# State space: phase tiles made in the first MLP and loaded, instead of sums in each period

## The chip, the cores and the metric

The kernel runs on one core of a Trainium2 chip. The metric is the device time of one execution in microseconds; the median of several runs is compared. The engines named below are TensorE (PE, with its weight loads as PEld), VectorE (DVE), ScalarE (ACT), GpSimd (POOL) and SyncE (SP), whose queue issues all transfers of this kernel.

## What is computed

The reference is a backbone of two layers over 1024 latent and 256 context tokens of width 1024: layer 0 mixes the tokens by attention, layer 1 by a bidirectional diagonal state space (S5); each mixer is followed by a squared-ReLU MLP. What matters here is the state space:

```
lam_bar = exp(lam * dt)
b_bar = ((lam_bar - 1.0) / lam)[..., None] * b_mat
bu = einsum('gpc,btgc->btgp', b_bar, uc)
a_cum, hs = associative_scan(_linear_combine, (a, bu))      # h[t] = lam_bar * h[t-1] + bu[t]
y = real(einsum('gcp,btgp->btgc', c_mat, hs))
```

lam_bar is complex. The kernel scans with its magnitude alone and takes the rotation out: before the scan the inputs are multiplied by the cosine and sine of a phase that grows with the position, and after the scan the products are turned back with the same cosine and sine. Eight tokens make one step, so that 1280 tokens are 160 positions. The phase of a position is held as a 32-bit integer, in which the full circle is 2 to the 32, and wraps by itself.

## The kernel before

The stages in question are the first MLP's down projection (`mlp0_start`, `mlp0_down`, about 1446 to 1906 us of the span), its end (`mlp0_end`, to about 1938), and the state space (`s5`, to about 2146).

**Down projection.** Eight blocks q of four hidden rows are multiplied into ten token tiles, in groups of tiles (2, 0, 1). After each tile `step` advances a list of background generators, `self.bg`, one or two yields at a time (L1538): first `s5_phases`, then `s5_tables`. `s5_tables` makes the matrices of the state space (loads of `tpd`, `tcd`, `tbd`; products on VectorE, L1138 to L1147; transposes and small products on TensorE, L1153 and L1159) and stores them to `recd`. Outside the stretches named below, a planner that estimates a timeline at build time fixes the order of each engine's instructions and of the transfers on SP's queue; on the chip each engine then runs its own list in that order.

**The phases.** The phase of position 16a + b of a column is the sum of a coarse and a fine table. `s5_phases` (L1198) loads the phase steps (`phd`), makes the fine table B (128 x 128 columns x 16) by doubling on GpSimd (L1207 to L1213), stores it, then makes the coarse table A (128 x 128 x 10) in the same SBUF, and stores it, both into `ptd`. These buffers lie in F from 40 KB on, where `s5_tables` puts its inputs afterwards. In `s5` both tables are loaded back: the columns of the first period into H (A0, B0), the whole, 13 KB a partition, into F from 42.5 KB.

**The state space** runs 16 periods n, of 4 groups of 16 columns each, and three more that only finish. There PE, DVE, ACT and POOL keep the order of the program (`manual`); SP's queue is ordered by the planner. In a period, for each direction d (0 forward, 1 backward):

- `phase` (L1677, the sum at L1681, on GpSimd) adds A and B for 4 columns into a 128 x 640 tile; `trig` (ScalarE, L1685 to L1688) makes sine and cosine of it;
- `inputs` (TensorE, L1701), `rotate` (VectorE, two products from PSUM, L1710), the sum of the two (GpSimd, L1791 forward, L1800 backward), `scan` (VectorE, L1719);
- `back` (L1727): for each direction one product on VectorE and one on GpSimd;
- `outputs` (TensorE, L1733, L1736), the GELU of the period two before (ScalarE, VectorE L1786, L1808), transposes (L1740), and, at periods 8, 10 and 12 to 17, half a segment of the modulation of layer 1 (L247 to L261) from 2 MB of weights loaded two periods earlier.

GpSimd's order in a period is `back` of the period before (backward), the phase sum of the next period forward, L1791, L1800, `back` forward, the phase sum of the next period backward:

```
back(pool, n - 1, 1, 1); phase(n + 1, 0)
pool.tensor_tensor(t1, t1, t2, ALU.add)     # L1791, after rotate(n, 0)
pool.tensor_tensor(t1, t1, t2, ALU.add)     # L1800, after rotate(n, 1)
back(pool, n, 0, 1); phase(n + 1, 1)
```

The tiles of sine and cosine are a ring of three pairs (`phs`). Each period loads its matrices (`load_x`, `load_w`, 2.1 MB) into one of two slots, `load_x` for two periods ahead, `load_w` for one.

Of the kernel before, what the change touches and what calls it, by code (L numbers as in the profile page):

```python
# [70 lines left out]
class Prog:  # L71
# [1125 lines left out]

    def s5_phases(self, o):  # L1198

        nc = self.nc  # L1200
        g = nc.gpsimd.tensor_tensor
        B, P, P16 = (self.fv(x, *d).bitcast(I32) for x, d in ((o, (128, 16)), (o + 8, (128,)), (o + 8.5, (128,))))
        self.dma(self.fv(o + 9, 128), self.phd)
        nc.vector.tensor_copy(P, self.fv(o + 9, 128))

        def fill(T, n, first):
            nc.gpsimd.memset(T[:, :, 0], 0)  # L1207
            g(T[:, :, 1], first, T[:, :, 0], ALU.add)
            m = 2
            while m < n:  # L1210
                g(T[:, :, m], T[:, :, m // 2], T[:, :, m // 2], ALU.add)
                e = min(2 * m, n)
                g(T[:, :, m + 1 : e], T[:, :, 1 : e - m], bcast(T[:, :, m], 2, e - m - 1), ALU.add)  # L1213
                m *= 2

        fill(B, 16, P)
        g(P16, B[:, :, 8], B[:, :, 8], ALU.add)
        self.dma(self.ptd[:, 5 * KB : 13 * KB], B.rearrange("p a b -> p (a b)"))
        yield
        A = self.fv(o, 128, 10).bitcast(I32)  # L1220
        fill(A, 10, P16)
        self.dma(self.ptd[:, 0 : 5 * KB], A.rearrange("p a b -> p (a b)"))
        yield


# [266 lines left out]
    def mlp0_start(self):  # L1492
# [10 lines left out]
        self.yb = Ring([self.PS[:, x : x + 1024] for x in (2048, 3072, 0)])  # L1503
        self.bg = [self.s5_phases(40), self.s5_tables(40, 0, self.bank(3), self.bank(2))]
        self.w2 = {}
# [134 lines left out]
    def s5(self):  # L1640
# [9 lines left out]
        rs = [[self.view(self.U, 52 + 5 * d + 2.5 * i, (4, 160)) for i in range(2)] for d in range(2)]  # L1650
        At, Bt = self.fv(42.5, 128, 10).bitcast(I32), self.fv(47.5, 128, 16).bitcast(I32)
        A0, B0 = self.hv(46, 2, 4, 10).bitcast(I32), self.hv(47, 2, 4, 16).bitcast(I32)
        phs = [(self.fv(x, 4, 160), self.fv(x + 2.5, 4, 160)) for x in (0, 7.5, 24.5)]
        ts = [[(self.fv(x, 4, 160), self.fv((12.5, 20)[d], 4, 160)) for x in ((5, 29.5), (15, 17.5))[d]] for d in range(2)]
# [21 lines left out]

        def phase(n, d):  # L1677

            x0, P = 64 * d + 4 * n, phs[(2 * n + d) % 3][0].bitcast(I32)
            a, b = (At[:, x0 : x0 + 4], Bt[:, x0 : x0 + 4]) if n else (A0[:, d], B0[:, d])  # L1680
            pool.tensor_tensor(P.rearrange("p x (a b) -> p x a b", b=16), bcast(a, 3, 16), bcast(b, 2, 10), ALU.add)  # L1681

        def trig(n, d):
            Ps, Pc = phs[(2 * n + d) % 3]
            act.activation(Pc, Ps.bitcast(I32), AF.Sin, scale=0.5 * UNPHASE)  # L1685
            act.activation(Ps, Ps.bitcast(I32), AF.Sin, scale=UNPHASE)
            act.activation(Pc, Pc, AF.Square)
            act.activation(Pc, Pc, AF.Copy, scale=-2.0, bias=1.0)  # L1688
# [14 lines left out]
        def rotate(n, d):  # L1703
            (Ps, Pc), (t1, t2) = phs[(2 * n + d) % 3], ts[d][n % 2]
            for j, (t, P) in enumerate(((t1, Pc), (t2, Ps))):
# [15 lines left out]
        def back(eng, n, d, j):  # L1721
            Ps, Pc = phs[(2 * n + d) % 3]
            o = cs[d][n % 2][j]
# [22 lines left out]

        for t, c0, w in ((A0, 0, 10), (B0, 5 * KB, 16)):
            self.dma(t, self.ptd[:, c0 : c0 + 128 * w].rearrange("p (d x w) -> p d x w", d=2, w=w)[:, :, 0:4])

        load_x(0)  # L1750
        self.dma(self.fv(42.5, 13 * KB).bitcast(I32), self.ptd)
        load_w(0)
        self.act_set("silu_and_others")
        with self.manual():
            act.activation(U[:, :, 160:192], U[:, :, 0:32], AF.Copy)
            for d in range(2):
                for i in range(2):
                    pool.memset(rs[d][i][:, :, 0:1], 0.0)
            phase(0, 0)
            phase(0, 1)  # L1760
            trig(0, 0)
# [3 lines left out]
            for n in range(19):  # L1765
# [5 lines left out]
                if 1 <= n <= 16:  # L1771
                    back(pool, n - 1, 1, 1)
                if gelu:
                    act.activation(u, y, AF.Square, scale=float(np.sqrt(0.044715)))
                if run:
                    trig(n, 1)
                    decay(n, 1)
                    inputs(n, 0)
                if 0 < n < 15:
                    phase(n + 1, 0)  # L1780
                if run:
# [15 lines left out]
                if run:  # L1797
# [4 lines left out]
                    if n == 0:  # L1802
                        phase(1, 0)
                        trig(1, 0)
# [11 lines left out]
                for i, (a, b) in enumerate(mods):  # L1816
                    if n == b:
                        self.ada_half_products(halves[i % 2 if i > 2 else 0], 1, 2 + i // 2, i % 2, self.PS[:, 1856:1984])
                if n + 1 < 16:
                    phase(n + 1, 1)  # L1820
                if 3 <= n < 19:
# [275 lines left out]
    def run(self):  # L2097
        tc = self.tc
        pool = lambda name, **kw: tc.tile_pool(name=name, bufs=1, **kw)
        with pool("cst") as self.cst, pool("psp", space=bass.MemoryType.PSUM) as psp, \  # L2100
# [12 lines left out]
            self.Ad = [dt(f"Ad{i}", 16, 128, 512) for i in range(7)]  # L2113
            self.phd, self.ptd = dt("phd", 128, 128), drp.tile([128, 13 * KB], I32, name="ptd")
            self.tcd, self.tbd, self.tpd = dt("tcd", 128, 128, 32), dt("tbd", 128, 128, 32), dt("tpd", 128, 128, 34)
# [99 lines left out]
```

## Time and profile before

| | us |
|---|---|
| three runs | 2986.51, 2996.61, 2990.26 |
| median | 2990.26 |
| span of the profiled execution | 2980.2 |
| down projection | 1446 to 1906 |
| its end | 1906 to 1938 |
| state space | 1938 to 2146 |

The profile is of one execution, and its span runs from the first to the last instruction; the page gives no other time for that execution. Times inside the trace count from the start of the span. Busy times are those of an engine's instructions; the granted clock of TensorE is a share of its full speed; the DMA share is the mean busy share of the core's 16 DMA engines. A row of a timeline has its start, its length, engine, line, operation, output and input, and, in brackets, how long the engine stood idle before it and what ended that.

### The profile page before, as it was taken

The numbers are of one execution on the slowest core, as the hardware profiler recorded it, in microseconds if no ns is written. First come the engines' busy times: TensorE is split into PE (matmuls) and PEld (weight loads), VectorE is DVE, ScalarE is ACT, GpSimd is POOL, SyncE is SP. The second block draws the span as 40 slices with busy tenths as digits, with TensorE's granted clock in tenths as the row PEclk, the third lists the DMA queues.
The fourth block names the chain that finished last, engine by engine and source line by source line (L and its number), as shares of the span: only waits on it lengthen the run. The fifth ranks groups of instructions, "written<-read, shape, count | busy, mean of one in ns | idle before, by whom it ended". The sixth has DMA issues, their size and how long they took to land.

```text
span 2980.2 us, 43413 instructions
## 1 busy us (share of the span) xinstructions
PE 2799.0 (94%) x15440; PEld 2335.0 (78%) x15440; DVE 1931.3 (65%) x2782; ACT 1314.3 (44%) x2406; POOL 1066.0 (36%) x923
## 2 busy tenths in 40 slices
PE   6998999999899999999999999688899899999999
PEld 4687887888777787888777778588788678888887
DVE  6356777777763654444577774799733687758566
ACT  3325655555553743333422232367534643334443
POOL 2314666666653600000100001589501543327323
PEclk9999999999999999999999999889999999999999
DMA  9955555555725446322666674568934244467544
GB/s 277 298 171 170 150 171 166 164 168 161 237 86 178 131 151 185 122 96 85 198 178 185 182 225 120 161 177 262 290 112 156 78 145 160 155 197 268 166 135 141
DMA packets 427941, 510.79 MB, mean 171 GB/s; under 512 B 59094, under 2 KB 304076, under 8 KB 426572
## 3 DMA queue, kind: packets, MB, share of 16 engines
q1 hardware_dynamic: 427724, 508.03, 55.8%
q8 instruction: 121, 1.98, 0.3%
q14 instruction: 96, 0.79, 0.1%
HBM read 353.38 MB, written 150.31 MB: 169 GB/s over the span
## 4 chain that ended last, share of the span: by engine, by line
PE 66%; DVE 9%; DMA 9%; issue 5%; POOL 4%; ACT 4%; SPq 2%; DVEq 0%; POOLq 0%; ACTq 0%
PE PS L132 19%; PE PS L134 19%; PE PS L133 19%; SPq L80 2%; PE PS L520 2%; PE PS L1701 2%; ACT F L543 2%; PE PS L1736 1%; DVE F L533 1%; PE PS L566 1%; PE PS L202 1%; DMA R<-Vd 1%; DMA H<-hidd 1%; DVE FD L1719 1%; DMA Kd<-R 1%
## 5 line engine op out<-in xcount | busy, mean ns | idle before, releaser
L132 PE MATMUL PS<-H,R 128*128 128x512 f32 (+1 forms) x840 | 311.4, 377 | 15.2 <-ACT F L579 13.5
L133 PE MATMUL PS<-H,R 128*128 128x512 f32 (+1 forms) x840 | 306.8, 365 | 5.2 <-POOL H L138 5.2
L132 PE MATMUL PS<-H 128*128 128x512 f32 x776 | 303.6, 393 | 3.9 <-ACT H L137 3.9
L134 PE MATMUL PS<-H,R 128*128 128x512 f32 (+1 forms) x840 | 306.3, 366 | 0.0
L133 PE MATMUL PS<-H 128*128 128x512 f32 x776 | 304.3, 392 | 0.0
L134 PE MATMUL PS<-H 128*128 128x512 f32 x776 | 302.6, 391 | 1.6 <-DVE H L138 1.6
L137 ACT ACTIVATE R<-W 128x512 fp32r<-128x512 f32 (+1 forms) x191 | 136.1, 717 | 195.0 <-PE PS L133 137.1
L132 PE MATMUL PS<-R,H 128*128 128x512 f32 x532 | 212.9, 403 | 2.9 <-ACT R L137 1.4
L543 ACT ACTIVATE F<-F,stat 128x1280 f32<-128x1280 f32 x128 | 174.4, 1362 | 84.7 <-DVE F L533 84.4
L134 PE MATMUL PS<-R,H 128*128 128x512 f32 x532 | 208.2, 395 | 1.9 <-DVE H L138 1.9
L133 PE MATMUL PS<-R,H 128*128 128x512 f32 x532 | 209.3, 394 | 0.0
L138 DVE TENSOR_TENSOR H<-W,H 128x512 fp32r<-128x512 f32 (+1 forms) x146 | 142.9, 988 | 101.0 <-ACT H L137 97.5
L138 DVE TENSOR_TENSOR R<-W,R 128x512 fp32r<-128x512 f32 (+1 forms) x154 | 141.7, 926 | 98.6 <-ACT R L137 78.7
L132 PEld LDWEIGHTS PS<-H,R 128*128 128x128 f32 x840 | 161.5, 193 | 41.5 <-ACT F L579 15.0
L533 DVE TENSOR_SCALAR_CACHE_REDUCE F<-PS 128x1280 f32<-128x1280 f32 x128 | 185.1, 1482 | 8.6 <-PE PS L520 8.3
L137 ACT ACTIVATE H<-W 128x512 fp32r<-128x512 f32 (+2 forms) x167 | 107.5, 653 | 180.5 <-PE PS L133 112.6
L133 PEld LDWEIGHTS PS<-H,R 128*128 128x128 f32 x840 | 163.0, 194 | 28.6 <-POOL H L138 6.8
L580 POOL TENSOR_SCALAR R<-F 128x256 fp32r<-128x256 f32 (+1 forms) x128 | 123.9, 968 | 169.3 <-ACT F L579 147.5
L134 PEld LDWEIGHTS PS<-H,R 128*128 128x128 f32 x840 | 162.5, 194 | 26.8 <-issue 1.2
L132 PEld LDWEIGHTS PS<-H 128*128 128x128 f32 x776 | 146.2, 189 | 36.8 <-ACT H L137 4.8
L134 PEld LDWEIGHTS PS<-H 128*128 128x128 f32 x776 | 146.2, 188 | 33.2 <-DVE H L138 2.5
L133 PEld LDWEIGHTS PS<-H 128*128 128x128 f32 x776 | 146.3, 189 | 30.7 <-issue 1.0
(443 smaller groups left out, 7307.6 us busy)
## 6 DMA issues: line engine op xcount, KB each, us to landing
W<-in_mlp_w SPq DMA_DIRECT2D x184, 256.0 KB
Ad<-F SPq DMA_DIRECT2D x112, 256.0 KB
W<-Ad SPq DMA_DIRECT2D x112, 256.0 KB
W<-in_ada_w SPq DMA_DIRECT2D x32, 512.0 KB
W<-in_mlp_w SPq DMA_DIRECT2D x32, 512.0 KB
H<-hidd SPq DMA_DIRECT2D x64, 256.0 KB
U<-in_ada_w SPq DMA_DIRECT2D x32, 512.0 KB
W<-in_s_w_glu SPq DMA_DIRECT2D x64, 256.0 KB
```

Source lines behind the costliest of these rows:

```text
L80: return self.nc.sync.dma_start(out=out, in_=in_)
L132: mm(out, ah, bh, start=first, stop=False, **kw)
L133: mm(out, ah, bl, start=False, stop=False, **kw)
L134: mm(out, al, bh, start=False, stop=last, **kw)
L137: self.nc.scalar.activation(hi, src, AF.Copy)
L138: (lo_eng or self.nc.vector).tensor_tensor(lo, src, hi.bitcast(F32), ALU.subtract)
L202: self.nc.tensor.matmul(acc[32 * j : 32 * j + 32, 0:256], self.scT[:, 2 * k : 2 * k + 32], w[:, 256 * j : 256 * j + 256], start=k == 0, st ...
L520: mm(self.PS[:, 1280 * c + k0 : 1280 * c + k1], Q[:, c, r, qs], K[c][:, k0:k1], start=r == 0, stop=r == 1)
L533: ts(p[c], self.PS[:, 1280 * c : 1280 * c + 1280], 1.0, None, ALU.mult, ALU.min, accum_out=sm[:, c : c + 1])
L543: nc.scalar.activation(p[c], p[c], AF.Exp, bias=sm[:, c : c + 1], scale=-1.0, accum_out=sn[:, 0:1] if c else s0[:, u + 1 : u + 2])
L580: nc.gpsimd.tensor_scalar(hi, t, 1.0, 0.0, ALU.mult, ALU.add)
L1701: mm(b[:, o : o + 160], X[:, d, i, 64 * j : 64 * j + 128], U[:, 4 * n + i, cols], start=True, stop=True)
```

## The change

`s5_phases` keeps both tables in SBUF (A no longer in the place of B) and stores neither. After them it makes all 32 phase tiles on GpSimd, 16 periods by 2 directions, in three buffers in W, and stores each to `ptd`, which becomes 16 x 2 x 128 x 640; it yields after every four tiles. In `s5` the loads of the tables and the sums of `phase` are gone. A load `load_ph` of a finished tile takes their place: the tiles of period 0 ahead of its matrices, (1, 0), (1, 1) and (2, 0) behind them, and in every period n from 1 on those of (n + 1, 1) and (n + 2, 0), after GpSimd's `back` of the period before in the program's order. The ring of sine and cosine grows from three pairs to five, in the place of the tables.

```diff
-    def s5_phases(self, o):
+    def s5_phases(self, o, w):
         nc = self.nc
         g = nc.gpsimd.tensor_tensor
-        B, P, P16 = (self.fv(x, *d).bitcast(I32) for x, d in ((o, (128, 16)), (o + 8, (128,)), (o + 8.5, (128,))))
-        self.dma(self.fv(o + 9, 128), self.phd)
-        nc.vector.tensor_copy(P, self.fv(o + 9, 128))
+        B, A, P, P16 = (self.fv(x, *d).bitcast(I32) for x, d in
+                        ((o, (128, 16)), (o + 8, (128, 10)), (o + 13, (128,)), (o + 13.5, (128,))))
+        self.dma(self.fv(o + 14, 128), self.phd)
+        nc.vector.tensor_copy(P, self.fv(o + 14, 128))
...
         fill(B, 16, P)
         g(P16, B[:, :, 8], B[:, :, 8], ALU.add)
-        self.dma(self.ptd[:, 5 * KB : 13 * KB], B.rearrange("p a b -> p (a b)"))
         yield
-        A = self.fv(o, 128, 10).bitcast(I32)
         fill(A, 10, P16)
-        self.dma(self.ptd[:, 0 : 5 * KB], A.rearrange("p a b -> p (a b)"))
         yield
+        made = Ring([self.wv(w + 2.5 * i, 4, 160).bitcast(I32) for i in range(3)])
+        for n in range(16):
+            for d in range(2):
+                x = slice(64 * d + 4 * n, 64 * d + 4 * n + 4)
+                t = made.next()
+                g(t.rearrange("p x (a b) -> p x a b", b=16), bcast(A[:, x], 3, 16), bcast(B[:, x], 2, 10), ALU.add)
+                self.dma(self.ptd[n, d], t.rearrange("p x n -> p (x n)"))
+            if n % 2:
+                yield
...
-        self.bg = [self.s5_phases(40), self.s5_tables(40, 0, self.bank(3), self.bank(2))]
+        self.bg = [self.s5_phases(40, 0), self.s5_tables(40, 0, self.bank(3), self.bank(2))]
...
-        phs = [(self.fv(x, 4, 160), self.fv(x + 2.5, 4, 160)) for x in (0, 7.5, 24.5)]
+        phs = [(self.fv(x, 4, 160), self.fv(x + 2.5, 4, 160)) for x in (42.5, 47.5, 0, 7.5, 24.5)]
+        ph = lambda n, d: phs[(2 * n + d) % 5]
...
-        def phase(n, d):
-
-            x0, P = 64 * d + 4 * n, phs[(2 * n + d) % 3][0].bitcast(I32)
-            a, b = (At[:, x0 : x0 + 4], Bt[:, x0 : x0 + 4]) if n else (A0[:, d], B0[:, d])
-            pool.tensor_tensor(P.rearrange("p x (a b) -> p x a b", b=16), bcast(a, 3, 16), bcast(b, 2, 10), ALU.add)
+        def load_ph(n, d):
+            self.dma(ph(n, d)[0].bitcast(I32).rearrange("p x n -> p (x n)"), self.ptd[n, d])
...
-        for t, c0, w in ((A0, 0, 10), (B0, 5 * KB, 16)):
-            self.dma(t, self.ptd[:, c0 : c0 + 128 * w].rearrange("p (d x w) -> p d x w", d=2, w=w)[:, :, 0:4])
-
+        load_ph(0, 0)
+        load_ph(0, 1)
         load_x(0)
-        self.dma(self.fv(42.5, 13 * KB).bitcast(I32), self.ptd)
         load_w(0)
+        for n, d in ((1, 0), (1, 1), (2, 0)):
+            load_ph(n, d)
...
-            phase(0, 0)
-            phase(0, 1)
...
                 if 1 <= n <= 16:
                     back(pool, n - 1, 1, 1)
+                for a in ((n + 1, 1), (n + 2, 0)):
+                    if n and a[0] < 16:
+                        load_ph(*a)
...
-                if 0 < n < 15:
-                    phase(n + 1, 0)
...
-                        phase(1, 0)
...
-                if n + 1 < 16:
-                    phase(n + 1, 1)
...
-            self.phd, self.ptd = dt("phd", 128, 128), drp.tile([128, 13 * KB], I32, name="ptd")
+            self.phd, self.ptd = dt("phd", 128, 128), drp.tile([16, 2, 128, 640], I32, name="ptd")
```

## Rows read from the trace of the kernel before

**Rows 1.** The page's chain that ended last, share of the span by engine:

```profile
PE 66%; DVE 9%; DMA 9%; issue 5%; POOL 4%; ACT 4%; SPq 2%; DVEq 0%; POOLq 0%; ACTq 0%
```

**Rows 2.** Windows: us, busy PE PEld DVE ACT POOL, PE clock, DMA share, GB/s

```profile
1446.00:1906.00 460.00, 456.11 (x2237) 364.78 (x2236) 321.97 (x413) 124.10 (x215) 46.22 (x50) 1.00 0.60 176
...
1938.00:2046.00 108.00, 90.79 (x705) 87.14 (x704) 100.94 (x93) 74.27 (x115) 99.98 (x54) 0.92 0.64 192
2046.00:2096.00 50.00, 44.07 (x438) 41.29 (x439) 48.86 (x49) 38.26 (x61) 46.26 (x26) 1.00 0.92 281
2096.00:2136.00 40.00, 35.92 (x424) 34.00 (x422) 37.76 (x43) 23.69 (x39) 29.48 (x16) 0.97 1.04 314
```

**Rows 3.** Timeline of VectorE, period 9 and the start of period 10:

```profile
2046.85 1.54 DVE L1710 TENSOR_TENSOR FD<-PS,FD 128x640 f32<-128x640 f32 x2
...
2050.97 1.48 DVE L1719 TENSOR_TENSOR_SCAN FD<-U,FD 128x640 f32<-128x640 f32 x1
...
2054.27 2.57 DVE L1719 TENSOR_TENSOR_SCAN FD<-U,FD 128x640 f32<-128x640 f32 x1
2056.88 1.58 DVE L1727 TENSOR_TENSOR FD<-FD 128x512 f32<-128x512 f32 x1
2058.38 1.54 DVE L1710 TENSOR_TENSOR FD<-PS,FD 128x640 f32<-128x640 f32 x2
```

**Rows 4.** Timeline of VectorE, the backward product of the last period:

```profile
2130.47 0.69 DVE L1727 TENSOR_TENSOR FD<-FD 128x512 f32<-128x512 f32 x1
```

**Rows 5.** Timeline of GpSimd, the same periods 9 and 15:

```profile
2053.76 1.74 POOL L1727 TENSOR_TENSOR FD<-FD 128x512 f32<-128x512 f32 x1
2055.57 2.34 POOL L1681 TENSOR_TENSOR FD<-FD 128x640 int32<-128x640 int32 x1
...
2059.68 1.28 POOL L1681 TENSOR_TENSOR FD<-FD 128x640 int32<-128x640 int32 x1
...
2130.61 1.69 POOL L1727 TENSOR_TENSOR FD<-FD 128x512 f32<-128x512 f32 x1 [1.52 <-PE PS L1740]
```

**Rows 6.** Timeline of VectorE, waits in the first periods; 1978.94 repeats the second:

```profile
1956.04 1.56 DVE L1710 TENSOR_TENSOR FD<-PS,FD 128x640 f32<-128x640 f32 x2 [2.54 <-ACT FD L1688]
...
1967.41 1.56 DVE L1710 TENSOR_TENSOR FD<-PS,FD 128x640 f32<-128x640 f32 x2 [0.35 <-ACT FD L1688]
```

**Rows 7.** Timeline of VectorE, the start of period 13:

```profile
2095.31 0.82 DVE L1710 TENSOR_TENSOR FD<-PS,FD 128x640 f32<-128x640 f32 x1 [0.97 <-ACT FD L1686]
```

**Rows 8.** Waits of SP's queue, 1930 to 2150: us in total, times, longest

```profile
SPq L80 <- PE PS L1701: 77.0, 18, 14.7
```

**Rows 9.** Timeline of GpSimd, tables of phases in the down projection:

```profile
1447.02 0.53 POOL L1208 TENSOR_TENSOR FD<-FD 128x128 int32<-128x128 int32 x1 [4.02 <-DVE FD L1204]
...
1463.06 0.34 POOL L1207 MEMSET FD<- 128x128 int32 x1 [9.26 <-DMA ptd<-FD]
...
1467.07 0.60 POOL L1213 TENSOR_TENSOR FD<-FD 128x128 int32<-128x128 int32 x1
```

**Rows 10.** Timeline of SP's queue, the stores of the tables and the first load behind:

```profile
1455.35 0.37 SPq L80 DMA_DIRECT2D ptd<-FD  x1
...
1467.70 0.33 SPq L80 DMA_DIRECT2D ptd<-FD  x1
1470.65 0.33 SPq L80 DMA_DIRECT2D FD<-tpd  x1
```

**Rows 11.** Timeline of VectorE, the first product of the state space's tables:

```profile
1473.51 0.76 DVE L1138 TENSOR_TENSOR FD<-FD 128x576 f32<-128x576 f32 x1 [10.67 <-DMA FD<-tcd]
```

**Rows 12.** Timeline of TensorE at the first small product of the tables:

```profile
1477.73 0.46 PE L1159 MATMUL PS<-FD 128*32 128x128 f32 x8 [2.04 <-DVE FD L1140]
...
1478.72 0.63 PE L134 MATMUL PS<-H 128*128 128x512 f32 x1
...
1481.81 0.39 PE L133 MATMUL PS<-H 128*128 128x512 f32 x1
```

**Rows 13.** DMA issues, 2100 to 2150, the largest kind: count, KB each

```profile
W<-recd SPq DMA_DIRECT2D x1, 768.0 KB
```

More of the change, by code (lines that the diff above doesn't have):

```diff
@@ L1650, in s5 @@
         rs = [[self.view(self.U, 52 + 5 * d + 2.5 * i, (4, 160)) for i in range(2)] for d in range(2)]
-        At, Bt = self.fv(42.5, 128, 10).bitcast(I32), self.fv(47.5, 128, 16).bitcast(I32)
-        A0, B0 = self.hv(46, 2, 4, 10).bitcast(I32), self.hv(47, 2, 4, 16).bitcast(I32)
-        phs = [(self.fv(x, 4, 160), self.fv(x + 2.5, 4, 160)) for x in (0, 7.5, 24.5)]
+        phs = [(self.fv(x, 4, 160), self.fv(x + 2.5, 4, 160)) for x in (42.5, 47.5, 0, 7.5, 24.5)]
+        ph = lambda n, d: phs[(2 * n + d) % 5]
         ts = [[(self.fv(x, 4, 160), self.fv((12.5, 20)[d], 4, 160)) for x in ((5, 29.5), (15, 17.5))[d]] for d in range(2)]
@@ L1675, in load_w @@
                 self.dma(b[64 * h : 64 * h + 64, 3072:4096], self.recd[n, 64 - 64 * h : 128 - 64 * h, 1536:2560])
-        def phase(n, d):
-            x0, P = 64 * d + 4 * n, phs[(2 * n + d) % 3][0].bitcast(I32)
-            a, b = (At[:, x0 : x0 + 4], Bt[:, x0 : x0 + 4]) if n else (A0[:, d], B0[:, d])
-            pool.tensor_tensor(P.rearrange("p x (a b) -> p x a b", b=16), bcast(a, 3, 16), bcast(b, 2, 10), ALU.add)
+        def load_ph(n, d):
+            self.dma(ph(n, d)[0].bitcast(I32).rearrange("p x n -> p (x n)"), self.ptd[n, d])
         def trig(n, d):
-            Ps, Pc = phs[(2 * n + d) % 3]
+            Ps, Pc = ph(n, d)
             act.activation(Pc, Ps.bitcast(I32), AF.Sin, scale=0.5 * UNPHASE)
@@ L1703, in rotate @@
         def rotate(n, d):
-            (Ps, Pc), (t1, t2) = phs[(2 * n + d) % 3], ts[d][n % 2]
+            (Ps, Pc), (t1, t2) = ph(n, d), ts[d][n % 2]
             for j, (t, P) in enumerate(((t1, Pc), (t2, Ps))):
@@ L1721, in back @@
         def back(eng, n, d, j):
-            Ps, Pc = phs[(2 * n + d) % 3]
+            Ps, Pc = ph(n, d)
             o = cs[d][n % 2][j]
```

## The prediction

> **What bounds the kernel now.** The chain that ended last is TensorE for two thirds of the span [rows 1]; a gain can only come from a stretch where it isn't, and a loss is certain where it is held up. So the stretches come next [rows 2]. The first MLP's down projection (1446 to 1906) is bound by TensorE, 456 of 460 us, with GpSimd idle nine tenths of it. In the state space (1938 to 2136) VectorE has the most work: 101 of 108, then 49 of 50 and 38 of 40 us, and GpSimd is nearly as full. The same rows show what else is short there: the DMA engines are 0.64 busy first, then 0.92 and 1.04.
>
> One period of the state space, line by line, shows why VectorE is full. Its instructions follow each other without a gap from 2046.85 to 2058.38, 11.53 us a period [rows 3]. Some are far longer than their like. The backward scan takes 2.57 us at 2054.27, the forward one 1.48; the product L1727 at 2056.88 takes 1.58, and 0.69 in the last period, which makes no phase sum [rows 3, 4]. Laid beside GpSimd's line [rows 5], the excess is always what GpSimd's instruction had left to run: the phase sum that began at 2055.57 ran to 2057.91, 1.03 us past the start of the product, which lost 0.89; the product of GpSimd from 2053.76 ran 1.23 us into the scan, which lost 1.09. In the other direction the phase sum takes 2.34 beside the scan, 1.28 alone. So the two engines exclude each other when both read SBUF operands, and a phase sum costs VectorE time though it is on another engine. The sum at 2059.68 stands beside VectorE instructions that read PSUM, 1.54 us a pair as elsewhere, and costs nothing.
>
> **The change, part by part.** (a) *Sums out of the periods.* Of the two a period, the one after GpSimd's L1727 holds VectorE: 1.58 - 0.69 = 0.89 us. It is there in periods 0 to 14, 15 x 0.89 = 13.4 us gained, on the path because VectorE has no gap. What is late next: the scan's 1.09 stays, since GpSimd's L1727 still stands before it. GpSimd's other L1727 now waits for the scan just as VectorE's does; had it gone first, it would hold VectorE 1.1 us instead. In the last period VectorE began first, 2130.47 against 2130.61 [rows 4, 5], so I take the 0.89; ends 0 and 0.89.
>
> (b) *Trigonometry early.* ScalarE no longer waits for sums. Near the start VectorE waited for it 2.54 us, then twice 0.35 [rows 6]: 3.2 us gained; nothing to 3.2.
>
> (c) Where VectorE is not the last, nothing is gained: in period 13 it waited 0.97 us for others [rows 7], so one 0.89 is taken off. (a) to (c): 13.4 + 3.2 - 0.9 = 15.7 us gained.
>
> (d) *Thirty tiles loaded in the periods* (two of the 32 come before). A tile is 128 x 640 x 4 bytes = 0.328 MB, at the 314 GB/s of the full stretch 1.04 us. The three loads of tables that fall away, 1.8 MB in all, lay before 1938. Up to 2046 there are 19 tiles, 20 us, and the engines were idle for 0.36 x 108 = 39 us [rows 2]: hidden. From period 9 on 11 tiles come, 11.5 us, and only 0.08 x 50 = 4.0 us was idle. To shorten this stretch by its six 0.89 = 5.3 us as well, the queue would have to find 11.5 - 4.0 + 5.3 = 12.8 us. The ends are 0 (the loads there run ahead of their use, and the tail goes on into the next stage) and 12.8. I take the middle, 6.4 lost: a tile is asked for one period ahead, about 11 us, and stands behind modulation halves of 2.1 MB, 6.7 us each, so some come late and some not. On SP's queue the second tile of a period waits for GpSimd's L1727 early in that period; the loads behind it wait for TensorE's inputs of the same period or later [rows 8], so that wait costs nothing.
>
> (e) *32 sums and stores in the down projection.* GpSimd's 32 x 1.28 = 41 us stand in 414 idle; even if each held VectorE in full, VectorE has 138 us idle there [rows 2]. The stores, 10.5 MB or 33 us of the queue, stand in 0.40 x 460 = 184 us idle. What is not free is the order. TensorE's order is fixed at build, and the tables' first product stands in it where the planner expected the tables. They use the same SBUF as the phases, so they start when the last phase is stored. Today the sums of table A run from 1463.06 to 1467.67, the store is issued at 1467.70, the loads go out at 1470.65, and VectorE begins at 1473.51 [rows 9 to 11]; TensorE had then waited 2.04 us at the first product, and ran slower right after, 0.63 us a matmul instead of 0.39 [rows 12]. The new chain drops the 9.26 us in which table A waited for B's store and adds 32 sums: 26.5 us from GpSimd's first add (1447.02) to VectorE becomes 26.5 - 9.3 + 32 x 1.36 = 61 us (1.36 is a sum with the gap between instructions). Lateness in proportion is 2.04 x 61 / 26.5 = 4.7, so 2.7 lost more than now. Its ends: a gain of 2.0 if the planner is exact, and 58 lost. For the latter: three buffers, each held for a sum, the issue and the landing of its store. Landing took 2.6 us for 0.66 MB (1467.70 plus 0.33 of issue to 1470.65) and 7.7 us behind other traffic for 1.05 MB (1455.35 to 1463.06) [rows 9, 10]. (1.28 + 0.33 + 2.6) / 3 = 1.4 us a tile, 45 us, hardly above GpSimd's own 43; (1.28 + 0.33 + 7.7) / 3 = 3.1, 99 us, 58 more than the bare sums. I stay by the low end, since a store is half of that A.
>
> (f) *Entry, 1906 to 1938.* Two sums of 1.3 us leave GpSimd, two small loads replace larger ones; the first rotation waits for TensorE, so zero. The cover gone, it would be the tiles' landing, 2 to 3 us.
>
> Sum: -15.7 + 6.4 + 2.7 = -6.6 us. The page gives the span of one profiled execution, 2980.2 us; the median of the three runs is 10.1 us above. The terms are differences within the span and are taken off the median: 2983.7, 0.2% less. A measurement of this kernel can tell some 0.3%, 9.0 us, from no change.
>
> **The rivals.** *The queue keeps up*: (d) is 0, the planner errs little: -15.7 + 2 = -13.7, 2976.6. For it: no wait on a load of the state space stands in today's critical stretch, though the queue is full. Against: eleven tiles more.
>
> *The queue becomes the bound* from period 9: the later stretch gains nothing and grows by 11.5 - 4.0 = 7.5; periods 0 to 8 keep 9 x 0.89 + 3.2 = 11.2; with (e), -11.2 + 7.5 + 2.7 = -1.0, 2989.3. The Trainium skill, page "DMA: Bandwidth & Descriptors", section Bandwidth, asks for transfers of 1 MiB or more for three quarters of the peak; by it a tile of 0.33 MB would cost more than its 1.04 us, which speaks for this rival. The trace speaks against the rule: the full stretch with 314 GB/s is made of smaller loads too, none above 0.8 MB [rows 13].
>
> *The tables come late* (the other side): one mechanism, at TensorE's first table product in the down projection. If the stores' landings pace the ring, TensorE stands still while the tables aren't there. It decides from 9.3 + 9.0 = 18.3 us of lateness, 32 tiles at 1.9 us instead of 1.36; at the middle of its bounds, 30, the time is 2990.3 - 9.3 + 30 = 3011. For it: 2.04 us of just that wait stand in the trace, and TensorE has no slack. Against: landings of 2.6 us.
>
> *It doesn't free VectorE*: GpSimd's L1727 takes the place of the sum before VectorE's. Then (a) is gone: 3.2 - 9.1, 5.9 us lost, 2996. Against it stands which of the two began first [rows 4, 5].
>
> **How the numbers follow.** Forecast 0.42, queue keeps up 0.34, tables late 0.13, queue bound 0.08, not freed 0.03. The forecast's own range is 2978 to 2992; 0.04 of its chance lies under -9 us, 0.02 above +9. Faster by over 0.3%: 0.34 + 0.04 = 0.38. Slower: 0.13 + 0.02, and 0.03 from the bound queue with dearer tiles: 0.18. Within: 0.44. Range: from all of 13.4 + 3.2 with a little of the entry, 2972, to a lateness of 23 us, 3004.
>
> **What would show it.** VectorE's L1727 of the backward direction at 0.69 instead of 1.58, and periods of 10.6 us up to period 8. From period 9 on ScalarE waits for landings of the tiles if (d) is right. The wait before the first L1159 on TensorE tells (e): some 5 us. If that wait is over 18, or the periods stay at 11.5, the forecast is wrong.

## The result and the profile after

| | us |
|---|---|
| before, 6 runs | 2990.53 (2986.51 to 2996.61) |
| changed, 6 runs | 3010.82 (3003.18 to 3021.63) |
| ratio | 1.0074, 95% interval 1.006 to 1.0089 |

The change costs 20.3 us. 2983.7 was forecast, with a range up to 3004: too low, and on the wrong side.

The two profiled executions lie at opposite ends: 2980.2 is below every run of before, 3019.8 belongs to the longest run of the changed kernel. The changed kernel was therefore profiled a second time (`changed_again`, below). A table by stage serves the whole text. Its boundaries are start times of rows: the first weight product of the down projection, the first rotation, the rotations that open periods 9 and 15, and the first weight product of the next stage. "Tables" is how long after its start the stage's first instruction of the matrices' tables (L1138) runs on VectorE; "idle" is the time in which TensorE stood still in the stage, up to 24 us before its end. "Down projection" thus reaches from the first weight product to the first rotation and takes in the end of that stage, in whose last 23 us TensorE has nothing to do in nearly every kernel.

| run | median | tables | down projection | idle | periods 0-8 | 9-14 | to next stage |
|---|---|---|---|---|---|---|---|
| before | 2990.5 | 39.1 | 504.3 | 5.5 | 108.2 | 73.6 | 29.5 |
| changed | 3010.8 | 83.3 | 527.5 | 25.3 | 98.8 | 89.0 | 35.0 |
| changed_again | 3010.5 | 82.2 | 523.9 | 21.4 | 96.9 | 79.1 | 34.2 |
| tiles_not_made | 2990.3 | 41.0 | 507.4 | 8.5 | 96.9 | 78.4 | 33.8 |
| making_only | 3006.4 | 85.3 | 520.4 | 16.7 | 107.5 | 75.7 | 29.0 |
| sums_only | 3003.1 | 69.7 | 517.9 | 16.0 | 107.2 | 74.0 | 30.0 |
| stores_on_pool | 2998.7 | 95.5 | 521.2 | 18.4 | 96.9 | 78.1 | 36.1 |
| sums_last | 2981.1 | 12.6 | 499.9 | 3.3 | 96.9 | 77.1 | 33.6 |
| sums_last_pool | 2987.7 | 12.6 | 507.5 | 9.8 | 96.5 | 79.5 | 35.4 |
| before_tables_first | 2982.1 | 12.4 | 500.3 | 2.6 | 107.5 | 73.7 | 30.3 |
| no_mod_loads | 2993.1 | 82.6 | 525.7 | 22.0 | 96.3 | 69.1 | 29.6 |
| loads_on_pool | 3009.9 | 81.7 | 523.4 | 20.6 | 98.8 | 74.5 | 36.3 |
| half_last_pool | 2981.9 | 12.3 | 498.8 | 2.6 | 100.5 | 75.6 | 33.5 |
| nine_tiles_last | 2975.4 | 12.9 | 497.8 | 1.8 | 100.9 | 74.0 | 30.0 |

By it the first profile loses 23.2 us in the down projection, gains 9.4 in periods 0 to 8, loses 15.4 in periods 9 to 14 and 5.5 after them; 5.9 of its longer span lie ahead of the stage, where both programs are alike. The second loses 19.6, gains 11.3, and loses 5.5 and 4.7.

The windows of the changed kernel that answer to [rows 2]: the first 100 us of the down projection, periods 0 to 8, periods 9 to 14, and the rest up to the next stage (length; busy time and count of TensorE, its weight loads, VectorE, ScalarE, GpSimd; granted clock; DMA share; GB/s).

```profile
1440.23:1540.23 100.00, 86.45 (x378) 70.19 (x379) 51.41 (x57) 33.06 (x50) 59.35 (x49) 0.93 0.71 234
1967.68:2066.51 98.83, 87.73 (x708) 84.14 (x708) 93.43 (x93) 66.97 (x105) 68.09 (x36) 0.97 0.87 252
2066.51:2155.48 88.97, 73.67 (x711) 70.07 (x711) 66.98 (x75) 54.78 (x88) 45.30 (x25) 0.90 1.04 290
2155.48:2190.44 34.96, 23.95 (x315) 21.87 (x313) 18.03 (x29) 12.11 (x22) 7.50 (x4) 0.84 0.88 272
```

TensorE lacks 13.5 of the first 100 us. VectorE is as full as before in the early periods and stands still for 22 of 89 us in the later ones, in which the DMA engines are at 1.04.

VectorE in the changed kernel at the end of period 5, to be laid beside [rows 3, 4]:

```profile
2026.96 1.41 DVE L1730 TENSOR_TENSOR FD<-FD 128x512 f32<-128x512 f32 x1
2028.29 2.56 DVE L1722 TENSOR_TENSOR_SCAN FD<-U,FD 128x640 f32<-128x640 f32 x1
2030.89 0.69 DVE L1730 TENSOR_TENSOR FD<-FD 128x512 f32<-128x512 f32 x1
```

The backward product is at 0.69 instead of 1.58; the scan before it still pays for GpSimd's product, 2.56. Now TensorE where it waits in the down projection, in the place of [rows 12]:

```profile
1523.54 0.80 PE L132 MATMUL PS<-RD,H 128*128 128x512 f32 x1 [9.55 <-DVE FD L1445]
1533.33 0.42 PE L1159 MATMUL PS<-FD 128*32 128x128 f32 x8 [3.99 <-issue]
```

The larger wait is not at the table product L1159 but ahead of it, for an evacuation (VectorE adds a finished product from PSUM to its sum in SBUF, which frees the PSUM bank). ScalarE and VectorE just before it:

```profile
1520.04 1.06 ACT L137 ACTIVATE H<-W 128x1024 fp32r<-128x1024 f32 x1 [19.60 <-DMA W<-in_mlp_w]
```

```profile
1521.12 1.23 DVE L138 TENSOR_TENSOR H<-W,H 128x1024 fp32r<-128x1024 f32 x1 [14.62 <-ACT H L137]
1522.27 1.22 DVE L1445 TENSOR_TENSOR FD<-PS,FD 128x1024 f32<-128x1024 f32 x1
1523.52 1.82 DVE L1138 TENSOR_TENSOR FD<-FD 128x576 f32<-128x576 f32 x1
```

The evacuation L1445 stands in VectorE's order behind the split of the next block's weights (L137 and L138 make a high and a low part of each), and those weights came late. Their loads stand on SP's queue among the stores of tiles. SP's two longest totals of waits there (1445 to 1570; us, times, longest):

```profile
SPq L80 <- POOL W L1227: 29.1, 22, 6.0
SPq L80 <- DVE H L138: 13.9, 16, 2.8
```

and GpSimd at the sums, in the place of [rows 9]:

```profile
1465.67 5.71 POOL L1227 TENSOR_TENSOR W<-FD 128x640 int32<-128x640 int32 x3
1476.79 11.31 POOL L1227 TENSOR_TENSOR W<-FD 128x640 int32<-128x640 int32 x9 [5.41 <-DMA ptd<-W]
...
1495.18 21.16 POOL L1227 TENSOR_TENSOR W<-FD 128x640 int32<-128x640 int32 x14 [1.70 <-DMA ptd<-W]
...
1521.28 5.18 POOL L1227 TENSOR_TENSOR W<-FD 128x640 int32<-128x640 int32 x3 [3.25 <-DMA ptd<-W]
```

The ring of three tile buffers makes GpSimd wait for landings now and then, and the sums run from 1465.67 to 1526.5. In the later periods VectorE's longest waits of the changed kernel are for ScalarE's trigonometry, and that waits for tiles (timeline, then the waits from 2066 to 2160):

```profile
2087.57 1.56 DVE L1713 TENSOR_TENSOR FD<-PS,FD 128x640 f32<-128x640 f32 x2 [7.59 <-ACT FD L1691]
2115.31 1.55 DVE L1713 TENSOR_TENSOR FD<-PS,FD 128x640 f32<-128x640 f32 x2 [4.91 <-ACT FD L1691]
```

```profile
ACT FD L1688 <- DMA FD<-ptd: 28.3, 6, 9.1
```

### The profile page after: what moved, and what is told of

Its sections match the earlier page's. It is cut to its first block, busy times and chain, and to the rows that moved or that the text cites. A ratio compares the mean times of both kernels' runs of the same rounds, so it can differ in the third digit from the quotient of the medians.

```text
span 3019.8 us, 43592 instructions
## 1 busy us (share of the span) xinstructions
PE 2809.6 (93%) x15440; PEld 2339.9 (77%) x15440; DVE 1931.5 (64%) x2782; ACT 1314.1 (44%) x2406; POOL 1048.6 (35%) x923
## 5 line engine op out<-in xcount | busy, mean ns | idle before, releaser
L137 ACT ACTIVATE R<-W 128x512 fp32r<-128x512 f32 (+1 forms) x191 | 136.2, 717 | 198.3 <-PE PS L133 143.3
L138 DVE TENSOR_TENSOR H<-W,H 128x512 fp32r<-128x512 f32 (+1 forms) x146 | 146.4, 1012 | 115.8 <-ACT H L137 113.3
L138 DVE TENSOR_TENSOR R<-W,R 128x512 fp32r<-128x512 f32 (+1 forms) x154 | 146.2, 956 | 93.5 <-ACT R L137 74.1
L137 ACT ACTIVATE H<-W 128x512 fp32r<-128x512 f32 (+2 forms) x167 | 107.4, 652 | 191.0 <-PE PS L133 109.1
L133 PEld LDWEIGHTS PS<-H 128*128 128x128 f32 x776 | 146.3, 189 | 30.3 <-issue 0.4
```

The costliest lines, as they stand in the source:

```text
L133: mm(out, ah, bl, start=False, stop=False, **kw)
L137: self.nc.scalar.activation(hi, src, AF.Copy)
L138: (lo_eng or self.nc.vector).tensor_tensor(lo, src, hi.bitcast(F32), ALU.subtract)
```

## The experiments

### Which half of the change costs

`tiles_not_made` leaves the down projection as before and changes the state space alone:

```diff
-            dma(ph(n, d)[0]..., self.ptd[n, d])
+            dma(ph(n, d)[0]..., self.ptd[:, 84 * (2 * n + d) : 84 * (2 * n + d) + 640])
...
+    def s5_phases(self, o):    # as before the change
```

> The state space is the changed one, with its 32 loads of 0.33 MB; the down projection is the old one: the two tables are made and stored, and each load takes a window of 128x640 words of the stored tables in place of a tile, so the phases are other numbers. No sum and no store of a tile is left. Theory (two losses, one in each place): from GpSimd's first instruction of the phases to the first rotation about 496 us as before; periods 0 to 8 about 99 us (108 before), periods 9 to 14 about 89 (74 before), the last period to the first matmul of the next stage 35 (30 before); in all some 10 us above the kernel before, about 3000. Rival (all of the loss is made in the down projection, and the long later periods are its echo): periods 9 to 14 at 64 to 74 us, in all 2974 to 2984.

Measured: ratio to before 0.9996 (0.9984 to 1.0008). The early periods gain 11.3 us, the later stretch loses 4.8 and 4.3, and the down projection, whose instructions are those of before, is 3.1 longer. The state space's part is worth nothing in sum; the 10 us expected of it were read from a profile whose later periods were unusually long.

`making_only` is the other half: tiles made and stored, tables stored as well, state space as before.

```diff
         fill(A, 10, P16)
+        self.dma(self.ptd[:, 0 : 5 * KB], A...)
...
-                self.dma(self.ptd[n, d], t...)
+                self.dma(self.ptt[n, d], t...)
```

> The down projection is the changed one, with 32 sums and 32 stores, and stores the two tables as well (1.8 MB more); the state space is the old one, which adds the tables in each period and never reads the stored tiles. Theory: from GpSimd's first instruction of the phases to the first rotation 510 to 519 us instead of 496, the state space 108 and 74 us as before; in all 10 to 23 above the kernel before, 3000 to 3013. Rival (the sums and stores hide in the down projection, the loss is the state space's alone): 496 us there, 2990 in all.

Measured: 1.0049 (1.0033 to 1.0065), 15.9 us above, as the theory said; the down projection is 16.1 longer, the state space as before. Most of the loss is made here.

### What in the making costs: the stores or the sums

`stores_on_pool`:

```diff
-                self.dma(self.ptd[n, d], t...)
+                nc.gpsimd.dma_start(out=self.ptd[n, d], in_=t...)
```

> The changed kernel, but GpSimd issues the 32 stores of tiles itself, so that no store stands on SP's queue. Theory (stores that wait for GpSimd hold the loads of the next block's weights behind them): SP waits no longer for GpSimd's sums, the weights come in time, the 9.6 us in which TensorE waited for VectorE's evacuation go; from the first instruction of the phases to the first rotation 500 to 508 us instead of 519, in all 11 to 19 below the changed kernel. Rival (the chain of sums makes the tables late, whatever queue stores them): 515 us or more, TensorE waits at the first table product or the evacuation instead, in all within 5 us of the changed kernel, about 3011.

Measured: 1.0032 (1.0019 to 1.0045). The median is 12 us below the changed kernel, inside what the theory gave, but the stage is hardly shorter in the trace, 521.2. Its first 100 us:

```profile
1439.33:1539.33 100.00, 100.00 (x441) 82.81 (x442) 54.98 (x52) 34.60 (x51) 73.50 (x80) 1.00 0.66 228
```

The early stall is gone, as the theory said. Yet TensorE stands still 18.4 us later in the stage, in smaller pieces. Two of them, at a transposition of the tables and at an evacuation:

```profile
1666.12 0.63 PE L1153 MATMUL PS<-ident,FD 128*128 128x128 f32 x4 [1.50 <-DVE FD L1147]
...
1900.27 0.50 PE L132 MATMUL PS<-RD,H 128*128 128x512 f32 x1 [3.81 <-DVE FD L1445]
```

The tables begin at 95.5, as GpSimd now also spends its time on issuing. So the theory named the first stall's immediate cause and not all that the stage loses. Where the 12 us of the median lie, the trace doesn't show: its execution was the longest of six (3004.4), that of `changed_again` the shortest of four (3003.4), and at these nearly equal times the stages are nearly equal too, 521.2 and 523.9.

`sums_only` takes the 32 stores out of `making_only`:

```diff
-                self.dma(self.ptt[n, d], t...)
```

> The kernel of the run in which the tiles were made and stored but not used (old state space, the tables stored and loaded), now without the 32 stores: GpSimd makes the 32 sums into the same three buffers and nothing takes them away. What is left of the change in the down projection is the later start of the matrices' tables. Theory (the larger part of the loss is the stores on SP's queue, which hold back the weights behind them; late tables cost less): TensorE has no wait of over 5 us for VectorE's evacuation; from the first product of the down projection to the first rotation 507 to 513 us (504 before, 520 with the stores), in all 3 to 9 above the kernel before, 2994 to 3001. Rival (late tables are most of it): 515 us or more, 3002 or more.

Measured: 1.0051 (1.0035 to 1.0067), 15.1 us above: nearly as much as with the stores. The rival is right. GpSimd makes the sums in one go, TensorE waits at the table product itself, and VectorE, before that, for one of the late sums (one fence for each engine):

```profile
1465.79 46.67 POOL L1229 TENSOR_TENSOR W<-FD 128x640 int32<-128x640 int32 x32
```

```profile
1519.12 0.66 PE L1159 MATMUL PS<-FD 128*32 128x128 f32 x8 [6.02 <-issue]
```

```profile
1509.51 3.57 DVE L1138 TENSOR_TENSOR FD<-FD 128x576 f32<-128x576 f32 x2 [3.64 <-POOL W L1229]
```

The tables use the memory of the phases and of the three tile buffers, so they wait for the sums with or without stores; SP's queue waited for GpSimd's sums 34.5 us here:

```profile
SPq L80 <- POOL W L1229: 34.5, 8, 6.4
```

### The tables first

`sums_last` swaps the two background generators of the changed kernel, and nothing else:

```diff
-        self.bg = [self.s5_phases(40, 0), self.s5_tables(...)]
+        self.bg = [self.s5_tables(...), self.s5_phases(40, 0)]
```

> The changed kernel with the two background generators of the down projection in the other order: the matrices' tables first, then the phase tables, the 32 sums and the 32 stores, in the same memory; the stores stay on SP's queue. The tables then wait for nothing of the phases. SP's queue has the hidden rows of the last two blocks standing between the stores. Theory (the large stall comes from loads that stand behind stores that wait for GpSimd, the smaller ones from late tables): the small ones go, a stall for the hidden rows comes near the end of the stage; from the first sum or table to the first rotation 500 to 512 us on the scale on which the kernel before has 496 and the changed one 519, in all 2994 to 3006. Rival (late tables are the whole loss there): 494 us, 2988 to 2992.

Measured: 0.9962 (0.9949 to 0.9975), 30 us below the changed kernel and 10 below before. The tables begin at 12.6, the stage takes 499.9, and TensorE's first table product stands without a wait:

```profile
1465.89 0.43 PE L1159 MATMUL PS<-FD 128*32 128x128 f32 x8
```

All 32 sums and stores are still there, with loads of hidden rows (the MLP's activations) standing between the stores on SP's queue; the stall that was expected of them did not come. What had cost time was that the tables stood behind the sums. The swap takes away both of the tables' waits, that for the shared memory and that for their place in the list; no run parts the two. Even 2981 is below what either theory gave, since both took the stage before the change as the measure.

`sums_last_pool` adds the edit of `stores_on_pool` to it.

> The same with the 32 stores issued by GpSimd. Theory: neither a late table nor a store before a load is left, so the down projection is as short as before the change or up to 4 us shorter; the state space stays as in the other runs with the changed one (97, 78 and 34 us), which is worth nothing in sum; in all 2985 to 2993, 18 to 26 below the changed kernel. Rival (the sums and stores cost VectorE or the DMA engines something wherever they are put): 5 us or more above that.

Measured: 0.9986 (0.9969 to 1.0003). The time is inside what was expected, but not the stage: 507.5, 7.6 more than with SP's queue. Of these, 2.9 are one wait of TensorE at a transposition of the tables, and 4.7 lie behind the last product of the down projection, where TensorE stood still for 28.0 us instead of 23.3:

```profile
1739.77 1.09 PE L1153 MATMUL PS<-ident,FD 128*128 128x128 f32 x4 [2.93 <-DVE FD L1147]
...
1946.67 6.64 PE L1704 MATMUL PS<-U,H 128*128 128x160 f32 x32 [27.99 <-issue]
```

GpSimd's last sum had ended at 1844.5, so its issuing, 0.55 us a store (below, in `stores_on_pool`), is not shown to be the cause of the larger part. The ten runs spread from 2972.9 to 2995.3, and the profiled one was 6.0 above their median. Why these waits grew stays open.

```profile
1485.55 1.10 POOL L1228 DMA_DIRECT2D ptd<-W  x2
```

`before_tables_first` is the control: the same swap in the kernel before.

> The kernel before with its two background generators in the other order and nothing else: the matrices' tables first, then the two phase tables. A control for the runs with the sums last. Theory (in the kernel before, too, the tables wait for the phases, and the first products on TensorE are late): from the first product of the down projection to the first rotation 498 to 501 us instead of 504, the state space as before, in all 3 to 6 below the kernel before, 2984 to 2988. Rival (what the runs with the sums last gained over the kernel before is the state space's alone): 2989 to 2992.

Measured: 0.9965 (0.995 to 0.998), 10.2 us below before, more than expected; the traces show 4.0 of it in the stage. Where the rest lies is not seen, as the profiled execution of before is itself some 8 us below the median of its runs. The gain of `sums_last` over before is the swap's: with it, 32 loaded tiles (2981.1) and sums in each period (2982.1) come out alike, as `tiles_not_made` and before do.

### What the later periods lose

`no_mod_loads` leaves out six of the eight loads of modulation weights.

```diff
-                    if n == a:
+                    if n == a and i in (0, 3):
                         self.ada_half_load(...)
```

> The changed kernel without six of the eight loads of modulation weights (2.1 MB each) in the state space: the products take the weights that lie in the buffers, so the modulation of layer 1 is wrong. Theory (from period 9 on the DMA engines are the bound): periods 9 to 14 fall from 89 to 64 to 68 us, VectorE waits no longer for ScalarE, the first matmul of the next stage comes 30 us after the last period's start; in all 25 to 30 below the changed kernel, 2981 to 2986. Rival (not the bytes but the place of the tiles' loads on SP's queue, behind loads that wait for TensorE, makes them late): periods 9 to 14 stay above 78 us.

Measured: 1.0009 (0.9999 to 1.0018), 18 us below the changed kernel and not 25 to 30; periods 9 to 14 take 69.1, just above the theory's 64 to 68 and far from the rival's 78. With 12.6 MB fewer, the DMA share of periods 9 to 14 falls to 0.88 and VectorE is full again:

```profile
2055.80:2124.88 69.08, 65.51 (x717) 62.80 (x716) 66.60 (x75) 55.05 (x88) 45.38 (x25) 1.00 0.88 250
```

From period 9 to the next stage it is 98.7 us, 4.4 less than before: the size of the six 0.89 less 0.9 of the prediction. VectorE's busy time there falls by 5.3, from 89.6 to 84.3; with six loads fewer the modulation waits less too, so the match is no proof.

`loads_on_pool` keeps the bytes and moves the tiles' loads off SP's queue.

```diff
                     if n and a[0] < 16:
-                        load_ph(*a)
+                        load_ph(*a, pool.dma_start)
```

> The changed kernel, but from period 1 on GpSimd issues the loads of tiles, right after its product that frees the buffer, so that they no longer stand on SP's queue behind the loads of matrices and modulation. The bytes are the same. Theory (bytes are the bound of the later periods): periods 9 to 14 stay at 76 to 89 us, in all within 6 us of the changed kernel, 3005 to 3016. Rival (the place on SP's queue): periods 9 to 14 fall to 65 to 71 us and the waits of ScalarE for tiles go, in all 10 to 20 below, 2991 to 3001.

Measured: 1.0054 (1.0037 to 1.007), 3009.9. Periods 9 to 14 take 74.5, between the theory's 76 to 89 and the rival's 65 to 71, but the rest grows to 36.3; the time is the theory's. The tiles come in time; now ScalarE and VectorE wait for the modulation's products instead (waits from period 9 to the next stage):

```profile
ACT adat L251 <- PE PS L247: 31.6, 6, 9.7
DVE modc L256 <- PE PS L254: 18.2, 3, 9.6
```

The same stretch of `changed_again` has these waits short, and the tiles' long:

```profile
ACT FD L1688 <- DMA FD<-ptd: 17.2, 5, 5.9
DVE FD L1713 <- ACT FD L1691: 11.6, 4, 4.5
...
ACT adat L251 <- PE PS L247: 10.0, 3, 6.7
...
DVE modc L256 <- PE PS L254: 6.7, 1, 6.7
```

So it is not the place on SP's queue that costs, and the bytes are left: periods 9 to 14 have a DMA share of 1.03 here, and the stretch gets shorter where bytes are taken out of it (`no_mod_loads` above, `nine_tiles_last` below). Why TensorE comes late to the modulation's products was not followed; only 1.9 us of it are a wait for their weights.

`half_last_pool` loads the backward tiles alone; the forward sums return to the periods (with the edit of `sums_last_pool`).

```diff
-            for d in range(2):
+            for d in range(1, 2):
...
+                if 0 < n < 15:
+                    phase(n + 1, 0)
```

> As the run before, but only the 16 tiles of the backward direction are made, stored and loaded; GpSimd adds the forward ones in the period, where VectorE reads PSUM, from the forward half of the tables. Half of the bytes (5.2 MB) leave the state space. Theory (VectorE's gain is the backward sum's alone, the later periods' loss is the bytes): VectorE's backward product stays at 0.69, periods 0 to 8 take 97 us, periods 9 to 14 66 to 71 instead of 78, the last period to the next stage's first weight product 30 to 32; in all 2974 to 2984, below both kernels. Rival (the loss in the later periods is not the bytes): periods 9 to 14 above 75 us, 2986 or more.

Measured: 0.9962 (0.9948 to 0.9975), below both kernels as expected, but periods 9 to 14 at 75.6 and not 66 to 71, which by itself is the rival's side. From period 9 to the next stage it takes 109.1 us, 6.0 more than before, for 6 tiles: 1.0 us a tile, and no gain from VectorE. So half the bytes is still too many, if the bytes are what costs; the next run settles that. The first periods are slower than with all tiles loaded, 100.5: the forward sum is back, and VectorE waits 1.86 us for trigonometry at the start (2.54 in before), while periods 4 to 7 keep 10.6.

### Both lessons together

`nine_tiles_last` takes tiles only where the queue has room: tables first, nine backward tiles (periods 0 to 8), sums in the periods otherwise.

```diff
-        for n in range(16):
-            for d in range(2):
+        for n in range(9):
+            for d in range(1, 2):
...
+                if n and n + 1 < 9:
+                    load_ph(n + 1, 1)
...
+                if 9 <= n + 1 < 16:
+                    phase(n + 1, 1)
```

> Tables first, then only the nine backward tiles of periods 0 to 8 made and stored (SP's queue) and loaded a period ahead; the forward sums, and from period 9 on the backward ones too, are made in the period as in the kernel before. So VectorE is freed where the DMA engines have room, and no tile's bytes fall where they have none. Theory: from the first product of the down projection to the first rotation 497 to 501 us; periods 0 to 8 97 to 101 (108 before), periods 9 to 14 72 to 75 as before, the last period to the next stage's first weight product 29 to 30; in all 2974 to 2980, below both kernels. Rival (the long later periods are not the tiles' bytes but follow from faster early periods, whose modulation and matrices are then asked for sooner): periods 9 to 14 77 us or more, 33 us after them, in all 2981 to 2988.

Measured: 2975.4, 0.9942 (0.9928 to 0.9957): 17 us below before, 6.7 below the swap alone. Periods 9 to 14 take 74.0 and the rest 30.0, as the theory has it: with faster early periods but no tile behind them the later stretch is as long as before, so the tiles made it longer. One trace now shows both forms, the backward products of period 7 (loaded tiles) and period 8 (the sum of period 9 beside it):

```profile
2021.94 0.69 DVE L1743 TENSOR_TENSOR FD<-FD 128x512 f32<-128x512 f32 x1
...
2032.59 1.58 DVE L1743 TENSOR_TENSOR FD<-FD 128x512 f32<-128x512 f32 x1
```

### The changed kernel once more

> The changed kernel as it is, for a profile of an execution nearer to its median (the one at hand was the longest of its six). Theory (each loss as the other runs with the same parts have it): from the first product of the down projection to the first rotation 522 to 528 us, periods 0 to 8 97 to 99, periods 9 to 14 76 to 82 instead of the 89 of the first profile, the last period to the next stage's first weight product 33 to 36; in all 3005 to 3015. Rival (the 89 us of the first profile are the rule, and belong to the made tiles): 86 us or more.

Measured: 3010.5, 1.0081 (1.0055 to 1.0107). Periods 9 to 14 take 79.1, as in the other kernels with the same state space (77.1 to 79.5); the 89.0 of the first profile is one execution's.

## Why the prediction was wrong

**(a) to (c), right.** The backward product is at 0.69, the early waits for trigonometry are gone. The working gives 9 x 0.89 + 3.2 = 11.2 us for periods 0 to 8; 9.4 to 11.9 were measured in the eight profiles with all 32 tiles loaded. The two runs that keep the forward sums, and with them the longest early wait, gain 7.7 and 7.3 there, near the 9 x 0.89 = 8.0 of (a) by itself. The rival "doesn't free VectorE" is out. The Trainium skill, page "SBUF — State Buffer", section "Who interferes with whom", says the same of a VectorE instruction with two SBUF inputs beside a GpSimd instruction that reads SBUF; the 0.69 and 1.58 of one trace agree.

**(d), the term was mis-sized.** "only 0.08 x 50 = 4.0 us was idle", and of the 12.8 "I take the middle, 6.4 lost", which beside the 4.4 gained there leaves 2.0 lost from period 9 to the next stage. Measured against the 103.1 of before: 7.6 to 11.8 lost (`sums_last`, `loads_on_pool`, `tiles_not_made`, `changed_again`, `stores_on_pool`, `sums_last_pool`), 20.9 in the first profile. The stretch followed its bytes alone: eleven tiles, 0.7 to 1.1 us each, and nothing of VectorE's gain. VectorE did have less to do, 84.8 us busy instead of 89.6 in the rows below, but it stood still for 28.5 instead of 13.5. "The queue becomes the bound", with 7.5, was right about this stretch; its chance was 0.08. One argument for it had been tiles that cost more than their share. They don't: from period 9 on `changed_again` moves 304 GB/s with tiles of 0.33 MB in it, before 295. The rule of the Trainium skill to batch to 1 MiB or more (page "DMA: Bandwidth & Descriptors", section Bandwidth) doesn't show here as a dearer tile. DMA engines that are busy 0.96 of the stretch, with the idle rest spread over it, had no 4 us to give.

```profile
2046.85:2149.93 103.08, 89.63 (x1023) 83.22 (x1022) 89.62 (x101) 66.09 (x108) 74.89 (x41) 0.97 0.96 295
```

```profile
2059.42:2172.71 113.29, 92.60 (x1027) 86.43 (x1025) 84.81 (x101) 66.61 (x109) 52.84 (x29) 0.93 1.01 304
```

The first row is before, the second `changed_again`.

**(e), the step that decided.** "Lateness in proportion is 2.04 x 61 / 26.5 = 4.7, so 2.7 lost". The stage lost 16.1 (`making_only`) to 23.2. Two things were wrong in it. The chain was not 61 us but 70.2, from GpSimd's first add (1453.28) to VectorE's first instruction of the tables (1523.52): with the landings a tile took 60.8 / 32 = 1.90 us, not 1.36. "I stay by the low end", 1.4 a tile for the ring, was too low. And the one wait of 2.04 was no measure of what late tables cost. In the built programs the first table product stands some 160 TensorE instructions later than before; at 100 us for the 441 of `stores_on_pool` that is 36 us, and it came 49.7 later (93.1 after the stage's start instead of 43.4). The 13.4 that the order lacked is the idle of the first 100 us, 13.5. Nearly twelve more stood idle afterwards (3.5 before), and the granted clock was 0.93 in these 100 us (0.98 before). Idle time makes 19.8 of the 23.2 lost. `stores_on_pool`, with an order that fitted, had none of the first stall and still a stage of 521. What goes with the stage's length in all fourteen profiles is when the tables begin: at 12 to 13 us 498 to 500 (507.5 with GpSimd issuing all 32 stores), at 39 to 41 504 to 507, at 70 518, at 82 to 96 520 to 528. The traces show where the later pieces stand: in `stores_on_pool`, of the waits over 0.3 us, 9.9 us at the tables' own transpositions and products (L1153, L1159) and 6.5 at three late evacuations; with the tables first, the former come to at most 3.3. Why late tables make these pieces stays open.

The sign that was named for (e), "some 5 us" before the first L1159, came in with 3.99 and was no sign: 9.55 stood at the evacuation ahead of it.

The rival "the tables come late" was thus right in its mechanism; the 1.90 us a tile is even the point from which it was to decide. That its 3011 was met is luck: it counted 30 us there and 9.3 gained elsewhere, where 16 to 23 were lost, and early gains of 11 were eaten by losses of some 10 in the later periods. And the landings were not needed for it: `sums_only`, with 32 bare sums in 46.7 us, lost 13.6 in the stage. Its place was half right, as the larger wait stood ahead of the table product.

**(f), right**: the first rotation waits 0.94 us for TensorE's inputs before and after, and TensorE stood still for 23.1 and 23.0 us ahead of them.

With the sizes as measured the sum is -11 + 10 + 20 = 19, against 20.3 between the medians.

## What to carry to other kernels

Work that is moved into an idle engine also takes the memory, the queue places and the start time of whatever comes after it there: ask first what waits for the moved work's buffers, and put the longer chain ahead (two generators swapped gave 10 us, where 32 sums in 414 us of idle had cost 16). In a stretch where the DMA engines are at 0.96, count each added tile at its full price and the faster engine's gain at nothing; take bytes only where there is room, which is what made nine tiles better than 32.

## What was not expected

The kernel before was itself 10 us slower than with its two generators swapped, though the largest wait of TensorE that the order left was one of 2.04 us. Moving loads from one queue to another in a full stretch changed who waited and left the time alone (3009.9 beside 3010.5). And with GpSimd issuing the stores, 0.55 us each beside a sum of 1.28, a schedule that otherwise had no stall came out 6.6 us slower (2987.7 beside 2981.1); the intervals of the two ratios overlap slightly, and with 16 such stores (`half_last_pool`) the stage took only 498.8, so the cause is not shown.
